# Expert biases split during w_o, slot lists read in one transfer per expert, six weight loads at the expert start, last tiles' routing in another order

## The chip, the cores and the metric

One core of a Trainium2 chip runs the whole layer. The metric is the device time of one execution in microseconds. The kernel before takes 2818.05 us, the median of three runs (2815.62 to 2819.49).

## The reference

Input x is (1, 1024, 1024): 1024 tokens of width 1024. After a mixer of two attention branches (a neighbourhood attention and a grouped-query attention), whose outputs are merged and multiplied by w_o, a mixture of experts follows. Cut to what the change touches:

```
x  = x + gt1 * rmsnorm(merge_branches(...) @ ..., g_post_mix)      # ends with the product by w_o
h2 = rmsnorm(x, g_pre_ffn) * (1 + sc2) + sh2
logits = h2 @ w_router + b_router                # 32 experts
top_logits, top_e = top_k(logits, 4)             # 4 experts for each token
top_w = softmax(top_logits)
for each expert e, for its tokens:               # 4096 assignments in all
    gu  = h2[tok] @ w_gu[e] + b_gu[e]            # 1024 x 2048
    act = (clip(gu_lin, -7, 7) + 1) * (min(gu_glu, 7) * sigmoid(1.702 * min(gu_glu, 7)))
    f[tok] += top_w * (act @ w_dn[e] + b_dn[e])  # 1024 x 1024
x  = x + gt2 * rmsnorm(f, g_post_ffn)
```

Everything is float32.

## The kernel before

A float32 product is made of three matmuls of a shorter type: each operand is split into hi and lo, and hi·hi, hi·lo and lo·hi are summed. ScalarE makes the hi of a weight piece (a copy, L1494), VectorE the lo (a subtraction, L1503).

The program runs through projections, attention, the product by w_o with the routing, the experts, and a final norm. A scheduler does not reorder it: each engine executes its instructions in the order in which the code issues them, and SP (SyncE) issues the DMAs of its queue in that order too. An instruction that waits holds back all that stands behind it on its engine.

**w_o and routing** (about 1000 to 1170 us). Eight tiles j of 128 tokens, each in two column chunks of 512 (ch = 0, 1). TensorE's product goes to a PSUM buffer z, and `evac` takes its sum of squares on ScalarE (L1203, Square) and multiplies it by a row on VectorE (L1205). An object `Post` carries a tile on in steps, which the loop interleaves with later tiles by a written list: s0 and s1 (norm, residual, the x2 store), s2 (second norm, the h2 store L1020), p0 (eight transposes of h2 and two copies to h2T, L1030), p1 (router product, L1036 and L1041, top four, softmax maximum), p2 (slot numbers), p3 (exponential L1277, weights, and four indirect DMAs from GpSimd, L1284, which write token and weight to their slots in DRAM, `slots_d`). For j from 4 to 6, tile j's list runs p1 of tile j−2, and p2 and p3 of j−3, behind its chunk 0, and s0 of j, p0 of j−1, then s1 and s2 of j behind its chunk 1. Behind tile 7's chunk 1 the rest has a list of its own.

**Experts** (about 1170 us to the end). 32 positions p. Even positions are wide experts (mode T, 304 slots at first, then fewer), odd ones narrow (64 or 128 slots). `slots(p)` reads which tokens an expert has from `slots_d`, by SP, one DMA for each 128 slots into buffers named slot, of which there are 12 (L1521), and for mode T a bias column (L1525). `gather(p)` fetches the token rows by an indirect DMA on GpSimd (L1534), `xtr(p)` transposes them (L1589). Steps U (gate and up, four for a position) and D (down, two) each take four weight pieces of 512 KB. A piece is loaded by SP (L1482) into one of 6 raw buffers, and split into 8 hi and 7 lo buffers. Between two wide experts steps alternate: U(p+1,0), U(p,2), U(p+1,1), U(p,3), U(p+1,2), D(p,0), U(p+1,3), D(p,1), D(p+1,0), U(p+2,0), D(p+1,1), U(p+2,1). The product of a T step is taken out of PSUM by ScalarE (gx, L1729) and VectorE (L1735). The output rows y are written back by indirect DMAs that take the token numbers from the slot buffer (f_d<-y, L1829).

`prepare(p)` calls `slots(p+2)`, `xtr(p)` and later `gather(p+1)`; it runs behind U(p−2,3) for even p and behind D(p−2,0) for odd p.

The biases of all experts (b_all, 32 rows of 3072) are needed from the first narrow step on, as hi in 32 partitions and lo in the next 32. At the expert start three DMAs on ScalarE's queue (L1852) read 1024 columns each, twice, into 64 partitions; ScalarE copies them to bhl (L1860) and VectorE subtracts (L1861).

Of the kernel before, what the change touches and what calls it, by code (L numbers as in the profile page):

```python
# [970 lines left out]
class Post:  # L971
# [22 lines left out]
    def s1(self):  # L994
        b, y = self.b, self.y
        nc, wk, V = b.nc, b.wk4, b.nc.vector
        r = self.r
        V.reciprocal(r[:, 1:2], r[:, 0:1])
        sq = b.w4.tile([P, D], F32, name="sq4", bufs=1)
# [38 lines left out]
    def p1b(self):  # L1038
        b, ps = self.b, self.lps
        for k in range(4, 8):  # L1040
            b.nc.tensor.matmul(ps[:, :32], self.hT[:, k, :], b.wr[:, k, :], start=False, stop=k == 7)  # L1041
        self.p2, self.p3 = b.route(self.t, ps)
# [6 lines left out]
class Tail(Build):  # L1049
# [65 lines left out]
    def phase4(self):  # L1115
# [56 lines left out]
        self.ctx3.close()  # L1172
        ws = ExitStack()
        wo["p"] = self.pool(ws, "wo")
        w4 = self.w4 = self.pool(es, "w4", 2, **R)
# [22 lines left out]
        def evac(ps, j, ch):  # L1198
# [3 lines left out]
            sq = w4.tile([P, D], F32, name="sq4", bufs=1)  # L1202
# [20 lines left out]
        for j in range(2, 8):  # L1223
            for ch in range(2):
                ps = self.tp4()
                for q in range(4):
                    gemm(ps, j, q, hl[8 + 2 * q + ch])
                evac(ps, j, ch)
                if ch == 0:
                    order = early.get(j, ((j - 2, "p1"), (j - 3, "p2"), (j - 3, "p3")))  # L1230
                elif j < 7:
                    order = ((j, "s0"),) + early.get(j + .5, ((j - 1, "p0"),)) + ((j, "s1"), (j, "s2"))
                else:
                    order = ((7, "s0"), (6, "p0"), (7, "s1"), (5, "p2"), (7, "s2"), (5, "p3"), (6, "p1"), (7, "p0"),
                             (7, "p1a"), (6, "p2"), (7, "p1b"), (6, "p3"), (7, "p2"), (7, "p3"))
# [9 lines left out]
    def route(self, t, ps):  # L1245
# [29 lines left out]
        def p3():  # L1275
            e4 = wk.tile([P, 4], F32, name="e4")
            nc.scalar.activation(e4, m8[:, 0:4], AF.Exp, bias=sm[:, 0:1], scale=1.0, accum_out=sm[:, 1:2])  # L1277
            data = wk.tile([P, 4, 2], F32, name="data")
# [10 lines left out]
        return p2, p3  # L1289
# [141 lines left out]
class Moe2(Tail):  # L1431
    def moe(self):
# [6 lines left out]
        es = self.early = ExitStack()  # L1439
        bhl = self.pool(es, "bia").tile([P, 3072], F32R, name="bhl")  # L1440
# [73 lines left out]
        def slots(p):  # L1514
            if p >= NE:
                return
            e = ereg("sync", p)
            SL[p] = []
            for a, n in tiles(p):
                sl = xgp.tile([P, 2], I32, name="slot", bufs=12)  # L1520
                nc.sync.dma_start(sl[:n], self.slots_d[ds(e * STRIDE + a, n), :])  # L1521
                SL[p].append(sl)
            if mode[p] == "T":
                b = xgp.tile([P, 24], F32, name="bcol", bufs=3)
                nc.sync.dma_start(b, A["b_col"][ds(e, 1)].rearrange("a p c -> p (a c)"))  # L1525
# [306 lines left out]
        def prepare(p):  # L1832
# [3 lines left out]
            slots(p + 2)  # L1836
            xtr(p)
# [7 lines left out]

        raw_b = []

        def load_biases():
            src = A["b_all"]
            for i in range(3):  # L1850
                r = wk.tile([P, D], F32, name="y5", bufs=3)
                nc.scalar.dma_start(r[:64], bass.AP(tensor=src.tensor, offset=src.offset + i * 1024,  # L1852
                                                    ap=[[0, 2], [3072, 32], [1, 1024]]))
                raw_b.append(r)

        def split_biases():
            G.memset(f(bhl[64:P]), 0.0)
            for i, r in enumerate(raw_b):
                cs = slice(i * 1024, i * 1024 + 1024)
                ACT.activation(bhl[0:64, cs], r[:64], AF.Copy)  # L1860
                V.tensor_tensor(out=bhl[32:64, cs], in0=r[32:64], in1=f(bhl[32:64, cs]), op=ALU.subtract)  # L1861
# [208 lines left out]
```

## Time and profile before

| | |
|---|---|
| median of three runs | 2818.05 us |
| the profiled execution | 2821.09 us |
| its span in the trace | 2819.5 us |
| mean granted TensorE clock | 0.977 of 2.4 GHz |
| TensorE busy | 2669.4 us (95%) |
| VectorE busy | 1958.6 us (69%) |
| ScalarE busy | 1591.3 us (56%) |
| GpSimd busy | 567.0 us (20%) |

TensorE's share of 95% is a mean. The page's second part cuts the span into 40 slices of 70 us and gives the busy tenths of each: only in the first slices, in slice 17 (about 1130 to 1200 us, between w_o and the experts) and in the last does TensorE fall under nine tenths, and in slice 17 its granted clock falls too.

```profile
PE   6899999999999999489999999999999999999993
PEclk9999999999999999699999999999999999999996
DMA  6224551502232343467787888888889889998896
```

### The profile page before, as it was taken

The numbers are of one execution on the slowest core, as the hardware profiler recorded it, in microseconds if no ns is written. First come the engines' busy times: TensorE is split into PE (matmuls) and PEld (weight loads), VectorE is DVE, ScalarE is ACT, GpSimd is POOL, SyncE is SP. The second block draws the span as 40 slices with busy tenths as digits, with TensorE's granted clock in tenths as the row PEclk, the third lists the DMA queues.
The fourth block names the chain that finished last, engine by engine and source line by source line (L and its number), as shares of the span: only waits on it lengthen the run. The fifth ranks groups of instructions, "written<-read, shape, count | busy, mean of one in ns | idle before, by whom it ended". The sixth has DMA issues, their size and how long they took to land. (4 is left out here: it accounts for less than half of the span.)

```text
span 2819.5 us, 44191 instructions
## 1 busy us (share of the span) xinstructions
PE 2669.4 (95%) x15564; PEld 2231.0 (79%) x15564; DVE 1958.6 (69%) x3148; ACT 1591.3 (56%) x2485; POOL 567.0 (20%) x495
## 2 busy tenths in 40 slices
PE   6899999999999999489999999999999999999993
PEld 3788887555677778488988899999999898998892
DVE  3722322777777546477877888888888888888895
ACT  3421212555577324356676666677677777777773
POOL 2310001666544222301011011011001100111001
PEclk9999999999999999699999999999999999999996
DMA  6224551502232343467787888888889889998896
GB/s 236 73 95 177 187 197 45 161 23 42 49 72 50 113 157 128 123 210 230 266 280 247 273 291 268 279 291 292 268 295 304 290 285 306 313 312 298 298 313 224
DMA packets 195618, 589.36 MB, mean 209 GB/s; under 512 B 48049, under 2 KB 54785, under 8 KB 195313
## 3 DMA queue, kind: packets, MB, share of 16 engines
q1 hardware_dynamic: 172443, 519.85, 54.4%
q0 software_dynamic: 19808, 65.27, 8.3%
q8 instruction: 123, 2.02, 0.3%
q10 hardware_dynamic: 3142, 1.40, 0.2%
q14 instruction: 102, 0.84, 0.1%
HBM read 528.74 MB, written 59.00 MB: 208 GB/s over the span
## 5 line engine op out<-in xcount | busy, mean ns | idle before, releaser
L1503 DVE TENSOR_TENSOR lo<-raw,hi 128x1024 fp32r<-128x1024 f32 x768 | 919.2, 1219 | 170.5 <-ACT hi L1494 74.8
L1494 ACT ACTIVATE hi<-raw 128x1024 fp32r<-128x1024 f32 x768 | 800.4, 1054 | 189.9 <-PE g L1657 82.9
L1657 PE MATMUL g<-xT,hi 128*128 128x320 f32 (+10 forms) x1792 | 518.2, 331 | 0.0
L1658 PE MATMUL g<-xT,lo 128*128 128x256 f32 x1792 | 483.6, 280 | 0.0
L1657 PEld LDWEIGHTS g<-xT,hi 128*128 128x128 f32 x1792 | 336.5, 188 | 10.8
L1658 PEld LDWEIGHTS g<-xT,lo 128*128 128x128 f32 x1792 | 338.4, 189 | 2.3
L1829 POOL DMA_INDIRECT f_d<-y,slot x34 | 59.9, 1762 | 1246.9 <-ACT y L1817 1105.4
L1657 PE MATMUL g<-aT,hi 128*128 128x288 f32 (+10 forms) x896 | 260.5, 333 | 0.0
L1658 PE MATMUL g<-aT,lo 128*128 128x256 f32 x896 | 241.9, 280 | 0.0
L1633 PE MATMUL g<-hi,xN 128*128 128x512 f32 x512 | 204.3, 399 | 0.0
L1634 PE MATMUL g<-lo,xN 128*128 128x512 f32 x512 | 202.4, 395 | 0.0
L174 DVE TENSOR_TENSOR wlo<-raw,whi 128x1024 fp32r<-128x1024 f32 x33 | 42.1, 1288 | 218.7 <-ACT whi L173 218.5
L1632 PE MATMUL g<-hi,xN 128*128 128x512 f32 x448 | 182.7, 408 | 0.0
L1657 PEld LDWEIGHTS g<-aT,hi 128*128 128x128 f32 x896 | 168.2, 188 | 5.2
L1658 PEld LDWEIGHTS g<-aT,lo 128*128 128x128 f32 x896 | 169.3, 189 | 0.6
L859 ACT ACTIVATE p<-S 128x512 f32<-128x512 f32 x160 | 94.2, 596 | 103.8 <-PE S L858 99.0
L613 DVE TENSOR_REDUCE mn<-S 128x1 f32<-128x512 f32 x180 | 100.8, 593 | 66.3 <-PE S L612 65.9
L400 PE MATMUL mm<-hTh,whi 128*128 128x512 f32 (+1 forms) x416 | 123.7, 385 | 1.7 <-ACT whi L173 1.7
L400 PE MATMUL mm<-hTh,wlo 128*128 128x512 f32 (+1 forms) x416 | 123.2, 383 | 0.0
L400 PE MATMUL mm<-hTl,whi 128*128 128x512 f32 (+1 forms) x416 | 123.0, 383 | 0.0
L1634 PEld LDWEIGHTS g<-lo,xN 128*128 128x128 f32 x512 | 96.4, 188 | 22.7
L1633 PEld LDWEIGHTS g<-hi,xN 128*128 128x128 f32 x512 | 96.4, 188 | 19.3
(413 smaller groups left out, 5804.0 us busy)
## 6 DMA issues: line engine op xcount, KB each, us to landing
raw<-in_w_gu_dram SPq DMA_DIRECT2D x509, 512.0 KB, 5.0
raw<-in_w_dn_dram SPq DMA_DIRECT2D x256, 512.0 KB, 4.5
raw<-in_w_mod_dram SPq DMA_DIRECT2D x40, 512.0 KB, 4.5
raw<-in_w_in_dram SPq DMA_DIRECT2D x34, 512.0 KB, 4.5
x<-in_x_dram SPq DMA_DIRECT2D x16, 512.0 KB, 5.4
sig_d<-stg POOLq DMA_DIRECT2D x16, 512.0 KB, 2.9
sig<-sig_d SPq DMA_DIRECT2D x8, 1024.0 KB, 4.9
kraw<-ka_d SPq DMA_DIRECT2D x16, 320.0 KB, 6.3
```

What stands on the lines that cost most here:

```text
L174: (G if i == 0 else V).tensor_tensor(out=lo, in0=r, in1=f(hi), op=ALU.subtract)
L400: T.matmul(ps[:, :n], w[:, ks], h[:, k, a:a + n], start=k == 0 and pi == 0, stop=k == KT - 1 and pi == 2)
L613: nc.vector.tensor_reduce(out=u.mn[:, i, j:j + 1], in_=ps[:, :n], op=ALU.min, axis=AX.X)
L859: nc.scalar.activation(u.p[t // 2][:, t % 2 * 512:t % 2 * 512 + 512], ps, AF.Exp, scale=-1.0)
L1494: ACT.activation(hi, raws[i], AF.Copy)
L1503: V.tensor_tensor(out=lo, in0=raws.pop(i), in1=f(his[pieces[i]]), op=ALU.subtract)
L1632: T.matmul(ps[:m], x[:, kk, P:P + m], hi[:, cs], start=False, stop=False)
L1633: T.matmul(ps[:m], x[:, kk, :m], hi[:, cs], start=False, stop=False)
L1634: T.matmul(ps[:m], x[:, kk, :m], lo[:, cs], start=False, stop=kk == 7)
L1657: T.matmul(ps[:, :2 * c], hi[:, cs], x[:, kk, :], start=first, stop=False)
L1658: T.matmul(ps[:, :256], lo[:, cs], x[:, kk, :256], start=False, stop=last)
L1829: G.indirect_dma_start(out=self.f_d, out_offset=bass.IndirectOffsetOnAxis(ap=SL[p][xi][:n, 0:1], axis=0), in_=Y[p][xi][:n], in_offset=None ...
```

## The change

- **Biases.** `biases(i)`, called behind the steps of tiles 3, 4 and 5, loads one third of b_all by SP, copies and subtracts; the bhl buffer is made before w_o. The DMA stands on SP behind the tile's h2 store, and on ScalarE the copy stands ahead of the next tile's Square. The scratch of the Squares (never read) moves to the ring "raw" of the earlier stage, from which the bias DMA's landing buffer is taken too.
- **Slot lists.** One DMA reads all slots of a position into one buffer of three columns, of which there are 5. The first two lists are read by GpSimd, behind the scatters; the bias columns have a function of their own on SP.
- **Expert start.** SP issues six weight loads at once; four rounds of hi, lo and a further load follow, then `prepare(0)`, then four hi and three lo.
- **Last tiles.** p3 is cut in two, the exponential (p3e) and the rest (p3d). Tile 5's exponential moves up behind tile 7's chunk 0; a dummy Exp behind s1 of tile 7 fixes where the activation table is loaded; p2 and the rest of p3 of tile 5 move ahead of s1 of tile 7, and p3 of tile 6 ahead of p1b of tile 7.

```
         sq = b.w4.tile([P, D], F32, name="sq4", bufs=1)      # before, in s1 and evac
+        sq = b.ring.tile([P, D], F32, name="raw")
...
+        def biases(i):
+            if i == 0:
+                G.memset(f(bhl[64:P]), 0.0)
+            src = A["b_all"]
+            r = self.ring.tile([P, D], F32, name="raw")
+            nc.sync.dma_start(r[:64], bass.AP(tensor=src.tensor, offset=src.offset + i * D,
+                                              ap=[[0, 2], [3072, 32], [1, D]]))
+            cs = slice(i * D, i * D + D)
+            ACT.activation(bhl[0:64, cs], r[:64], AF.Copy)
+            V.tensor_tensor(out=bhl[32:64, cs], in0=r[32:64], in1=f(bhl[32:64, cs]), op=ALU.subtract)
...
                 if ch == 0:
                     order = early.get(j, ((j - 2, "p1"), (j - 3, "p2"), (j - 3, "p3")))
+                    if j == 7:
+                        order += ((5, "p3e"),)
...
-                    order = ((7, "s0"), (6, "p0"), (7, "s1"), (5, "p2"), (7, "s2"), (5, "p3"), (6, "p1"), (7, "p0"),
-                             (7, "p1a"), (6, "p2"), (7, "p1b"), (6, "p3"), (7, "p2"), (7, "p3"))
+                    order = ((7, "s0"), (6, "p0"), (5, "p2"), (5, "p3d"), (7, "s1"), (7, "s2"), (6, "p1"), (7, "p0"),
+                             (7, "p1a"), (6, "p2"), (6, "p3"), (7, "p1b"), (7, "p2"), (7, "p3"))
                 for t, x in order:
                     getattr(tiles[t], x)()
+                    if (t, x) == (7, "s1"):
+                        ACT.activation(self.spacer2, self.eps[0:1], AF.Exp)
...
+                if ch == 1 and 3 <= j <= 5:
+                    biases(j - 3)
...
-        def slots(p):
+        def slots(p, eng="sync"):
...
-            for a, n in tiles(p):
-                sl = xgp.tile([P, 2], I32, name="slot", bufs=12)
-                nc.sync.dma_start(sl[:n], self.slots_d[ds(e * STRIDE + a, n), :])
+            e, nt = ereg(eng, p), len(tiles(p))
+            sl = xgp.tile([P, 3, 2], I32, name="slot", bufs=5)
+            getattr(nc, eng).dma_start(sl[:, :nt], self.slots_d[ds(e * STRIDE, nt * P), :].rearrange("(a p) c -> p a c", p=P))
+            SL[p] = [sl[:, i] for i in range(nt)]
...
-        load(2)
-        slots(0)
+        load(N_RAW)
+        slots(0, "gpsimd")
         gather(0)
-        load(3, "gpsimd")
-        split_hi(2)
-        split_lo(2)
-        load_biases()
-        slots(1)
+        slots(1, "gpsimd")
+        columns(0)
+        for _ in range(4):
+            split_hi()
+            split_lo()
+            load()
         prepare(0)
         while cold or chains:
             advance()
-        load(2)
-        split_hi(3)
+        split_hi(4)
         split_lo(3)
-        split_biases()
-        split_hi(3)
-        split_lo(2)
```

**ScalarE in w_o.** The first piece is ScalarE's order before, from tile 3's second norm (the Square of y, its square root) over the two Squares of tile 4's chunks to tile 3's h2T. "waits" names the engines or DMA lanes whose semaphore an instruction waits for.

```order
L1004 ACTIVATE sq4_9300,s24_9301<-y_9164 128x1024 [waits DVE_49,Activation_49]
L982 ACT_TABLE_LOAD
L982 ACTIVATE r4_9307<-s24_9301,eps_8243 128x1 [waits Activation_49]
L1203 ACTIVATE sq4_9341,ss_9338<-z_9312 128x512 [waits PE_49]
L1277 ACT_TABLE_LOAD
L1277 ACTIVATE e4_9376,sm_9261<-m8_9251,sm_9261 128x4
L1203 ACTIVATE sq4_9415,ss_9338<-z_9390 128x512 [waits PE_49,Activation_49]
L982 ACT_TABLE_LOAD
L982 ACTIVATE r4_9420<-s4_9418,eps_8243 128x1 [waits DVE_49]
L1030 ACTIVATE h2T_9422<-z_9423 128x512 [waits PE_49]
```

The same place after the change:

```order
L1004 ACTIVATE raw_9305,s24_9306<-y_9168 128x1024 [waits DVE_49]
L982 ACT_TABLE_LOAD
L982 ACTIVATE r4_9312<-s24_9306,eps_8243 128x1 [waits Activation_49]
L1191 ACTIVATE bhl_8848<-raw_9318 64x1024 [waits DMAHW0_49]
L1222 ACTIVATE raw_9351,ss_9348<-z_9322 128x512 [waits PE_49]
L1303 ACT_TABLE_LOAD
L1303 ACTIVATE e4_9269,sm_9266<-m8_9256,sm_9266 128x4
L1222 ACTIVATE raw_9425,ss_9348<-z_9400 128x512 [waits PE_49,Activation_49]
L982 ACT_TABLE_LOAD
L982 ACTIVATE r4_9430<-s4_9428,eps_8243 128x1 [waits DVE_49]
L1030 ACTIVATE h2T_9432<-z_9433 128x512 [waits PE_49]
```

The copy to bhl, which waits for a DMA lane, now stands between tile 3's square root and the Square of tile 4's first chunk; the square root of tile 4 and the h2T copies of tile 3 follow behind it.

**SP late in the pair of positions 4 and 5.** Before, SP's queue around the slot read for position 9 (slot) and the weight loads behind it:

```order
L1482 DMA raw5_13739<-in_w_dn_dram 128x1024 [waits DMAHW6_49,DVE_49]
L1482 ISA
L1482 DMA raw5_13752<-in_w_gu_dram 128x1024 [waits DMAHW7_49,DVE_49,Activation_49]
L1460 TENSOR_LOAD erow_10005
L1460 ISA x2
L1521 ISA
L1521 DMA slot_13763<-slots_d_103 128x2 [waits DMASW5_49,DMASW2_49]
L1482 ISA
L1482 DMA raw5_13798<-in_w_gu_dram 128x1024 [waits DMAHW0_49,DVE_49]
L1482 ISA
L1482 DMA raw5_13827<-in_w_gu_dram 128x1024 [waits DMAHW1_49,DVE_49]
```

And after the change:

```order
L1509 DMA raw5_13737<-in_w_gu_dram 128x1024 [waits DMAHW1_49,DVE_49,Activation_49]
L1509 ISA
L1509 DMA raw5_13750<-in_w_gu_dram 128x1024 [waits DMAHW2_49,DVE_49]
L1487 TENSOR_LOAD erow_10023
L1487 ISA x2
L1546 ISA
L1546 DMA slot_13761<-slots_d_103 128x2 [waits DMASW3_49,DMASW4_49,DMASW0_49,Activation_49]
L1509 ISA
L1509 DMA raw5_13796<-in_w_gu_dram 128x1024 [waits DMAHW3_49,DVE_49]
L1509 ISA
L1509 DMA raw5_13825<-in_w_gu_dram 128x1024 [waits DMAHW4_49,DVE_49]
```

One more weight load stands ahead of the read than before. The read's waits (DMASW lanes, GpSimd's DMAs) are before those of scatters of older positions; after the change they are the lanes of the scatters of position 4, whose slot buffer it takes, and of ScalarE.

**ScalarE behind it.** Before, the split of the first weight piece loaded behind that read (raw5_13798) and the gx evacuation of step U(6,0):

```order
L1494 ACTIVATE hi5_13748<-raw5_13739 128x1024 [waits DMAHW4_49,DVE_49]
L1573 ACTIVATE xN_13765<-t5_13788 128x4x128 [waits PE_49]
L1494 ACTIVATE hi5_13794<-raw5_13752 128x1024 [waits DMAHW5_49,DVE_49]
L1573 ACTIVATE xN_13765<-t5_13817 128x4x128 [waits PE_49]
L1494 ACTIVATE hi5_13823<-raw5_13798 128x1024 [waits DMAHW7_49,DVE_49]
L1494 ACTIVATE hi5_13850<-raw5_13827 128x1024 [waits DVE_49,DMAHW0_49,PE_49,Activation_49]
L1729 ACTIVATE gx_13864<-g5_13770,bcol_12184 128x224 [waits PE_49]
L1729 ACTIVATE gx_13864<-g5_13770,bcol_12184 128x224
L1729 ACTIVATE gx_13875<-g5_13771,bcol_12184 128x224 [waits PE_49]
```

And after the change, where that piece is raw5_13796:

```order
L1601 ACTIVATE xN_13763<-t5_13786 128x4x128 [waits PE_49]
L1521 ACTIVATE hi5_13792<-raw5_13737 128x1024 [waits DMAHW7_49,DVE_49]
L1601 ACTIVATE xN_13763<-t5_13815 128x4x128 [waits PE_49]
L1521 ACTIVATE hi5_13821<-raw5_13750 128x1024 [waits DMAHW0_49,DVE_49]
L1521 ACTIVATE hi5_13848<-raw5_13796 128x1024 [waits DVE_49,DMAHW2_49,PE_49,Activation_49]
L1757 ACTIVATE gx_13862<-g5_13768,bcol_12184 128x224 [waits PE_49]
L1757 ACTIVATE gx_13862<-g5_13768,bcol_12184 128x224
L1757 ACTIVATE gx_13873<-g5_13769,bcol_12184 128x224 [waits PE_49]
L1757 ACTIVATE gx_13873<-g5_13769,bcol_12184 128x224
```

The split of the first piece behind the read, which waits for its DMA, now stands directly ahead of the gx evacuation; before, one other split stood between.

## Rows read from the trace of the kernel before

**Rows 1.** Windows: us, busy of each engine (instructions), TensorE's clock, DMA share, GB/s.
```profile
1094.00:1102.10 8.10, 8.10 (x42) 6.81 (x42) 4.14 (x19) 2.86 (x6) 4.60 (x9) 1.00 0.40 130
1208.00:1216.00 8.00, 4.58 (x34) 4.34 (x32) 2.83 (x3) 3.45 (x4) 0.00 (x0) 1.00 0.22 84
2500.00:2589.00 89.00, 89.00 (x585) 80.59 (x584) 78.49 (x108) 67.64 (x101) 8.82 (x8) 1.00 0.90 309
```
**Rows 2.** Timeline, TensorE: start us, us, engine, line, operation, out<-in, count, idle before.
```profile
1142.13 0.40 PE L1194 MATMUL z<-wo15h,zl 128*128 128x512 f32 x1
...
1195.90 0.62 PE L1660 MATMUL g<-xT,hi 128*128 128x304 f32 x1
...
1236.59 0.40 PE L1624 MATMUL g<-bhl,oneh 128*128 128x512 f32 x1
```
**Rows 3.** Timeline of one w_o tile, SP, ScalarE and TensorE.
```profile
1094.20 0.32 SPq L1020 DMA_DIRECT2D h_d<-h  x1
...
1100.14 0.60 ACT L1203 ACTIVATE sq<-z 128x512 f32<-128x512 f32 x1 [5.21 <-PE z L1194]
...
1102.34 1.06 ACT L1030 ACTIVATE h2T<-z 128x512 f32<-128x512 f32 x2
...
1106.29 0.97 PE L1036 MATMUL z<-wr,h2T 128*128 128x32 f32 x8
...
1114.30 0.60 ACT L1203 ACTIVATE sq<-z 128x512 f32<-128x512 f32 x1 [5.42 <-PE z L1194]
```
**Rows 4.** Timeline, ScalarE, the third bias copy.
```profile
1212.55 1.06 ACT L1860 ACTIVATE bhl<-y 64x1024 fp32r<-64x1024 f32 x1 [5.79 <-DMA y<-in_b_all_dram]
```
**Rows 5.** DMA, 1176 to 1178 us, ScalarE's queue: packets, MB, share of sixteen engines.
```profile
q10 hardware_dynamic: 18, 0.07, 13.0%
```
**Rows 6.** DMA issues, whole span: count, KB each, median us to landing.
```profile
raw<-in_w_gu_dram SPq DMA_DIRECT2D x509, 512.0 KB, 5.0
...
raw<-qb_d SPq DMA_DIRECT2D x16, 256.0 KB, 3.5
```
**Rows 7.** Timeline, hand-over from routing to the first expert.
```profile
1159.18 0.98 POOL L1284 DMA_INDIRECT slots_d<-data,sl  x1 [3.92 <-DVE sm L1280]
...
1168.08 0.97 POOL L1284 DMA_INDIRECT slots_d<-data,sl  x1 [0.22 <-issue]
...
1172.60 1.61 SPq L1521 DMA_DIRECT2D slot<-slots_d  x3
...
1175.45 1.00 POOL L1534 DMA_INDIRECT xg<-h_d,slot  x1 [6.40 <-DMA slot<-slots_d]
...
1182.27 0.88 POOL L1534 DMA_INDIRECT xg<-h_d,slot  x1 [0.67 <-issue]
...
1191.96 0.63 PE L1589 MATMUL t<-ident,xg 48*128 48x48 f32 x4 [0.59 <-DMA xg<-h_d,slot]
```
**Rows 8.** Timeline, ends of positions 2 and 26.
```profile
1445.12 0.39 PE L1657 MATMUL g<-xT,hi 128*128 128x512 f32 x1
...
1445.79 1.73 POOL L1829 DMA_INDIRECT f_d<-y,slot  x1 [6.65 <-ACT hi L1494]
...
2587.72 0.33 SPq L1521 DMA_DIRECT2D slot<-slots_d  x1
...
2596.60 1.33 POOL L1829 DMA_INDIRECT f_d<-y,slot  x1 [7.71 <-DVE lo L1503]
...
2598.59 0.65 ACT L1729 ACTIVATE gx<-g,bcol 128x144 f32<-128x144 f32 x2
...
2605.22 0.30 PE L1657 MATMUL g<-xT,hi 128*128 128x288 f32 x1
```
**Rows 9.** DMA issues at those two scatters: count, us to landing.
```profile
f_d<-y,slot POOLq DMA_INDIRECT x1, 5.0
...
f_d<-y,slot POOLq DMA_INDIRECT x1, 6.9
```
**Rows 10.** The scatters' line (L1829) over the span.
```profile
DMA to landing us min/median/max: 3.1/8.8/11.3
```

More of the change, by code (lines that the diff above doesn't have):

```diff
@@ L998, in s1 @@
         V.reciprocal(r[:, 1:2], r[:, 0:1])
-        sq = b.w4.tile([P, D], F32, name="sq4", bufs=1)
+        sq = b.ring.tile([P, D], F32, name="raw")
         s2 = wk.tile([P, 2], F32, name="s24", bufs=4)
@@ L1041, in p1b, with p3 @@
             b.nc.tensor.matmul(ps[:, :32], self.hT[:, k, :], b.wr[:, k, :], start=False, stop=k == 7)
-        self.p2, self.p3 = b.route(self.t, ps)
+        self.p2, self.p3e, self.p3d = b.route(self.t, ps)
+    def p3(self):
+        self.p3e()
+        self.p3d()
     def p1(self):
@@ L1172, in phase4 @@
         self.ctx3.close()
+        self.early = ExitStack()
+        bhl = self.bhl = self.pool(self.early, "bia").tile([P, 3072], F32R, name="bhl")
         ws = ExitStack()
         wo["p"] = self.pool(ws, "wo")
+        def biases(i):
[8 more added lines that the diff above has]
+            V.tensor_tensor(out=bhl[32:64, cs], in0=r[32:64], in1=f(bhl[32:64, cs]), op=ALU.subtract)
         w4 = self.w4 = self.pool(es, "w4", 2, **R)
@@ L1201, in evac @@
             y, ss = tiles[j].y, tiles[j].ss
-            sq = w4.tile([P, D], F32, name="sq4", bufs=1)
+            sq = self.ring.tile([P, D], F32, name="raw")
             ACT.activation(sq[:, :512], ps, AF.Square, accum_out=ss[:, ch:ch + 1])
@@ L1273, in p2, with p3e, p3d @@
             V.tensor_tensor(out=self.cum, in0=self.cum, in1=mk[:, None, :].to_broadcast([P, 2, 32]), op=ALU.add)
-        def p3():
-            e4 = wk.tile([P, 4], F32, name="e4")
+        e4 = wk.tile([P, 4], F32, name="e4")
+        def p3e():
             nc.scalar.activation(e4, m8[:, 0:4], AF.Exp, bias=sm[:, 0:1], scale=1.0, accum_out=sm[:, 1:2])
+        def p3d():
             data = wk.tile([P, 4, 2], F32, name="data")
@@ L1288, in p3 @@
                     self.tc.declare_no_dep(self.scat[-1].ins, o.ins, reason="slots of other assignments")
-        return p2, p3
+        return p2, p3e, p3d
     def counts(self, wk):
@@ L1438, in moe @@
         N_HI, N_LO, N_RAW = 8, 7, 6
-        es = self.early = ExitStack()
-        bhl = self.pool(es, "bia").tile([P, 3072], F32R, name="bhl")
+        es, bhl = self.early, self.bhl
         rawp = self.pool(es, "raw5", N_RAW)
@@ L1512, in tiles, with columns @@
             return [(a, min(P, c - a)) for a in range(0, c, P)]
-        def slots(p):
+        def slots(p, eng="sync"):
             if p >= NE:
                 return
-            e = ereg("sync", p)
-            SL[p] = []
-            for a, n in tiles(p):
-                sl = xgp.tile([P, 2], I32, name="slot", bufs=12)
-                nc.sync.dma_start(sl[:n], self.slots_d[ds(e * STRIDE + a, n), :])
-                SL[p].append(sl)
-            if mode[p] == "T":
+            e, nt = ereg(eng, p), len(tiles(p))
+            sl = xgp.tile([P, 3, 2], I32, name="slot", bufs=5)
+            getattr(nc, eng).dma_start(sl[:, :nt], self.slots_d[ds(e * STRIDE, nt * P), :].rearrange("(a p) c -> p a c", p=P))
+            SL[p] = [sl[:, i] for i in range(nt)]
+        def columns(p):
+            if p < NE and mode[p] == "T":
                 b = xgp.tile([P, 24], F32, name="bcol", bufs=3)
-                nc.sync.dma_start(b, A["b_col"][ds(e, 1)].rearrange("a p c -> p (a c)"))
+                nc.sync.dma_start(b, A["b_col"][ds(ereg("sync", p), 1)].rearrange("a p c -> p (a c)"))
                 BC[p] = b
@@ L1836, in prepare @@
             slots(p + 2)
+            columns(p + 2)
             xtr(p)
@@ L1843, in prepare @@
             cold.append(then())
[L1846 to L1861, printed above, removed]
-        load(2)
-        slots(0)
-        gather(0)
-        load(3, "gpsimd")
-        split_hi(2)
-        split_lo(2)
-        load_biases()
-        slots(1)
+        load(N_RAW)
+        slots(0, "gpsimd")
+        gather(0)
+        slots(1, "gpsimd")
[4 more added lines that the diff above has]
+            load()
         prepare(0)
```

## The prediction

> **What bounds the kernel now.** I read the windows first, then TensorE's timeline over the joint between two stages, then the chain through one w_o tile, one hand-over and one pair of experts, and last the DMA issues. In the w_o stage TensorE is busy 8.10 of 8.10 us while VectorE is busy 4.14, and late in the expert stage it is busy 89.00 of 89.00 us with the DMA engines at 0.90 [rows 1]. So in both stages TensorE sets the time, and whatever makes it wait is paid whole. Between them it idles: w_o's last matmul is at 1142.13, the first expert product at 1195.90 [rows 2]. That joint is a chain of latencies (scatter of slots, slot read, gather, transpose), and there the change can win. The first two expert steps are slow too: 40.7 us (1195.90 to 1236.59, [rows 2]) for 192 matmuls; at the pace of the second window, 34 in 4.58 us busy or 0.135 each [rows 1], they need 25.9.
>
> **A. The expert start.** Before, six raw buffers fill in two lots, and three of the loads stand on GpSimd's queue behind the gathers; now all six go out on SP as soon as the buffers exist, and four are split ahead of the first transposes. The bias copy, which before still waited for its transfer at 1212.55 [rows 4] with the splits of weights queued behind it on ScalarE, is gone from here. Of the 14.8 us lost in the first two steps I keep 3 for TensorE's slower clock after idling and for the first loads, and take 11.8 as gained.
> The rest is the slot path. Tile 6's scatters began at 1159.18, 3.92 us after the queue fell empty, and eight in a row ended at 1169.05 (1168.08 + 0.97). With tile 6's routing put ahead of tile 7's half I estimate that the run starts 2.7 us sooner (most of the 3.92) and ends at 1166.3. From the scatters' end the slot read took 3.6 to issue (1172.60) and 2.9 more to the first gather (1175.45): now about 1172.8. The third gather was issued 6.8 after the first, since each waited for its own slot list; with one list the three follow each other at about 1 us, so the third goes at 1174.8 and, with the same 9.7 to landing (1182.27 to 1191.96), lands at 1184.5 [rows 7]. Ten weight loads, 5.2 MB, now run beside it, for which I take 1.5 back: 1186, so 6 us sooner. Sum of A: −18, from −12 (the gathers starve beside the loads) to −23 (they do not, and the clock costs nothing).
>
> **B. The biases in w_o.** Per transfer: one DMA, one ScalarE copy of 1.06 [rows 4], one VectorE subtract, about 1.2. The work itself lies beside TensorE. The wait does not: ScalarE runs in program order, and the copy stands directly ahead of the Square that evacuates the next product, with a wait on the transfer. The transfer is issued behind the h2 store at 1094.20 [rows 3], so at about 1094.55. When does it land? The trace shows the same access on ScalarE's queue: 18 packets in 2 us at 13.0% of sixteen engines, that is 9 per us on 2.1 engines [rows 5]. 256 KB in 4 KB packets are 64, so 7.1 us, and I add 2.6 for start and completion, near the 2.85 from a slot read's issue to the gather that waits for it [rows 7]: 9.7. The bounds are 3.5, which a 64-partition load of the same size took [rows 6], and 14, if the 0.40 that other traffic takes of the DMA engines in w_o [rows 1] comes off its rate.
> The Trainium skill, "DMA: Bandwidth & Descriptors", section "Why a DMA increments its semaphore by 16 and not by 1", says that a DMA uses as many engines, up to 16, as divide the slowest dimension of both sides; the source's is 2 here, and the trace's 2.1 engines agree. The same page's "Anatomy of one DMA" fits 2.0 us plus bytes over 436 GB/s, an estimate of 2.6 us for 256 KB, and by it B would be nothing; the 9 packets per us speak against it.
> What is late: from landing, the copy 1.06, the subtract 1.2, VectorE's row of evacuation and routing (4.4: the 4.14 of the first window [rows 1] and small gaps), the square root 0.3 and the two h2T copies 1.06 [rows 3] make 8.1, with hand-overs 8.3. TensorE's router product read h2T at 1106.29 [rows 3]; now h2T is ready at 1094.55 + 9.7 + 8.3 = 1112.55: a stall of 6.3, or landing time minus 3.4. For the next two tiles the chain closes on itself. From the h2T copies' start (1102.34) to the next bias transfer are 6.4 (1094.55 plus the period 14.16 between 1100.14 and 1114.30, [rows 3]). A round is 9.7 + 8.3 − 1.06 + 6.4 = 23.3 against 14.16: 9.1 more, twice. Sum of B: 6.3 + 18.2 = 24.5, taken as +25; with landing in 3.5 it is 0 to 6 (the rounds 3 longer each), with 14 it is +37.
>
> **C. Slot lists in five buffers.** Before there were twelve buffers of 128 rows; now five, each for a whole expert. The read for position p+5 takes over the buffer of p, and p's scatters read their row numbers there until they have landed. For even p this read is issued just after p's last output step. SP issues in order, so it stands still until the last scatter of p has landed, and the weight loads stand behind it. In SP's order the wait changes from old scatters to the newest ones, and in ScalarE's order the split of the next load stands directly ahead of the gx evacuation. There are 14 such reads (positions 5, 7, ... 31).
> The price at p = 26: SP reached the read at 2587.72; the last scatter began at 2596.60 and landed 6.9 later, 2603.5 [rows 8, 9]. From there the next load needs 0.6 to issue, 5.0 to land [rows 6], its ScalarE split 1.06, and then, ScalarE being in order, the gx evacuation 0.65 [rows 8] that frees the product's PSUM buffer, with some 0.5 of VectorE: 7.8. TensorE wanted that buffer at 2605.22 [rows 8]; 2603.5 + 7.8 = 2611.3, so 6 late. Done so for all 14: 2.9 for the first, 13.6 for the second (1445.79 + 5.0 + 7.8 against 1445.12, [rows 8, 9]), 5.3 on average for twelve, together 80. But while SP stands still no weights fly, and scatters land faster: the fastest took 3.1 against a median of 8.8 [rows 10]. I take 3.8 off the landing and 0.5 off the first load's: 0 for the first, 9 for the second, 1 for each of the twelve. Sum of C: +20, from 5 (only the second pair shows) to 80.
>
> The tail's remaining swaps (an exponential earlier, one activation-table load more) lie in A's chain and are in its 2.7. Scratch for the squares moved to another ring: nothing, since it is written and never read, unless ScalarE waits for a raw weight in it (under 1).
>
> **Sum.** −18 + 25 + 20 = +27 on the profiled execution's 2821.09 (span 2819.5): 2848. That execution lies 3.0 above the median of the three runs, 2818.05; so **2845**.
>
> **Rivals.**
> 1. Only the gain shows: the bias transfer lands within 3.5 us (for it: the 64-partition load; against: the row of 9 packets per us), and scatters land so fast without weights that SP loses nothing (for it: 3.1; against: the second scatter of a tile still starts some 9 us after SP arrives). 2818 − 18 = 2800. Faster.
> 2. The scatters land no faster, so C costs its 80: for it, packets of loads already queued still run; 2818 − 18 + 25 + 80 = 2905. This is the slow end.
> 3. C is hidden, six raw buffers carrying TensorE across: 2818 − 18 + 25 = 2825. Against it: TensorE waits not for the load but for the evacuation behind its split.
> 4. B is hidden, C as forecast: 2818 − 18 + 20 = 2820, no change that a measurement of this kernel can tell (within 0.2%, 5.6 us).
>
> **Chances.** Forecast 0.60, rival 1 0.15, rival 2 0.10, rival 3 0.08, rival 4 0.07. Slower by over 0.2% takes the forecast, rival 2 and some of 3, less a little for a forecast whose terms come out low together: 0.73. Within 0.2%: 0.09. Faster: rival 1 and a little of the rest, 0.18. The forecast's own range, from the bounds taken moderately, is 2822 to 2890; half of rival 1 goes in at the lower end, rival 2 stays out: 2800 to 2890.
>
> **What would show it.** A: first expert product near 1215 (1195.90 − 6 + 25), and steps U(0,0) and U(0,1) in about 29 us. B: three gaps of TensorE in w_o ahead of the router product of tiles 3, 4, 5, of 6 to 9 us, and ScalarE idle ahead of the bias copy released by the bias DMA; landing near 9.7. C: SP's wait of 5 to 10 us at every second slot read released by a scatter, a dip in weight traffic, and TensorE gaps at the second step of even positions, large at position 4. I am wrong if these gaps are absent, above all if the bias lands within 4 us, or if scatters landing early let SP go on before TensorE needs the buffer.

## The result, and the profile after

The changed kernel takes 2958.08 us (median of 6 runs, 2948.71 to 2962.04) against 2818.89 us for the kernel before on the same chip: ratio 1.0489, 95% interval 1.0471 to 1.0506. The forecast was slower, 2845 us, with a range to 2890: the direction was right, the size was not. The profiled execution spans 2956.1 us against 2819.5, so 136.6 us are to be found.

The page of the kernel after, second part, in slices of 74 us:

```profile
PE   6999999999999997699899999999999899999993
PEclk8999999999999997799999999999999999999996
```

TensorE's tenths hide it: the slices of the expert stage read 9 and 8 where they were 9. The windows of one long stretch tell more. Columns as in [rows 1]; first the kernel after, then the kernel with six slot buffers (below), whose TensorE, VectorE and ScalarE are busy there as long as before to within 0.4%. Behind the bounds stand the length, the busy time of TensorE, of its weight loads, of VectorE, ScalarE and GpSimd, then TensorE's granted clock, the DMA share and GB/s:

```profile
1500.00:2700.00 1200.00, 1124.95 (x6668) 1021.13 (x6667) 929.73 (x1233) 784.60 (x1149) 107.57 (x77) 0.97 0.82 265
```
```profile
1500.00:2700.00 1200.00, 1193.90 (x7315) 1084.19 (x7314) 1014.23 (x1344) 864.83 (x1259) 122.05 (x87) 1.00 0.88 290
```

TensorE lies idle for 75 of 1200 us instead of 6, the DMA engines carry 265 instead of 290 GB/s, and the granted clock is 0.97 instead of 1.00.

**w_o.** The kernel after, timeline of SP, ScalarE and TensorE around the first bias, to be held against [rows 3], and TensorE's two later waits and its last product of w_o (before at 1142.13, [rows 2]):

```profile
1095.18 0.65 SPq L1188 DMA_DIRECT2D raw<-in_b_all_dram  x1
...
1105.38 1.06 ACT L1191 ACTIVATE bhl<-raw 64x1024 fp32r<-64x1024 f32 x1 [12.17 <-DMA raw<-in_b_all_dram]
...
1112.81 1.92 PE L1036 MATMUL z<-wr,h2T 128*128 128x32 f32 x8 [5.75 <-ACT h2T L1030]
...
1134.75 1.51 PE L1036 MATMUL z<-wr,h2T 128*128 128x32 f32 x8 [3.41 <-ACT h2T L1030]
...
1156.56 1.92 PE L1036 MATMUL z<-wr,h2T 128*128 128x32 f32 x8 [4.18 <-ACT h2T L1030]
...
1168.61 0.40 PE L1213 MATMUL z<-wo15h,zl 128*128 128x512 f32 x1
```

Windows of the same trace, while ScalarE stands at the bias copy and behind each of the three waits:

```profile
1100.50:1105.30 4.80, 4.80 (x27) 4.07 (x26) 0.00 (x0) 0.00 (x0) 0.00 (x0) 1.00 0.13 51
...
1112.80:1116.00 3.20, 3.19 (x15) 3.19 (x16) 2.85 (x4) 1.89 (x4) 2.92 (x4) 0.50 0.45 160
1134.70:1138.00 3.30, 3.25 (x18) 3.25 (x18) 2.94 (x4) 1.93 (x4) 2.93 (x4) 0.58 0.43 162
1156.50:1160.00 3.50, 3.44 (x17) 3.45 (x17) 3.15 (x4) 2.87 (x8) 2.98 (x5) 0.50 0.40 150
```

ScalarE stands 12.17 us at the bias copy, which starts 10.2 after the transfer's issue; late in that time the DMA engines are at 0.13 of sixteen, or 2.1 engines. TensorE waits three times, 13.3 us in all, and the eight router matmuls behind each wait take 1.5 to 1.9 us instead of 0.97: the granted clock there is 0.50 to 0.58, all or most of the time the lower of its two levels (1.2 of 2.4 GHz). w_o ends 26.5 us later; 25.9 of them come between its first product and its last (112.9 us instead of 87.0).

**The hand-over.** The kernel after, GpSimd (last scatter, first slot list, first and third gather) and TensorE's first expert product, against [rows 7] and [rows 2]:

```profile
1192.44 0.97 POOL L1312 DMA_INDIRECT slots_d<-data,sl  x1 [0.22 <-issue]
...
1198.78 0.82 POOL L1546 DMA_DIRECT2D slot<-slots_d  x1 [5.38 <-ACT hi L1521]
...
1204.77 1.00 POOL L1562 DMA_INDIRECT xg<-h_d,slot  x1 [5.17 <-DMA slot<-slots_d]
...
1207.34 0.88 POOL L1562 DMA_INDIRECT xg<-h_d,slot  x1 [0.30 <-issue]
```
```profile
1217.86 0.62 PE L1688 MATMUL g<-xT,hi 128*128 128x304 f32 x1
...
1247.12 0.40 PE L1652 MATMUL g<-bhl,oneh 128*128 128x512 f32 x1
```

The gathers follow each other at 1.3 us instead of spreading over 6.8, but the first begins 12.3 after the last scatter's start, not 7.4. From w_o's last product to the first expert product are 49.3 us (53.8 before), and the first two steps take 29.3 (40.7 before). The three gathers land after 4.4 to 6.1 us, where before they took 9.1 to 9.6.

**A pair of experts.** The kernel after at the end of position 20, GpSimd, SP, ScalarE and TensorE, to be held against [rows 8], and the landing of that scatter, after and before:

```profile
2424.49 1.36 POOL L1857 DMA_INDIRECT f_d<-y,slot  x1 [8.20 <-DVE lo L1530]
...
2428.16 0.34 SPq L1546 DMA_DIRECT2D slot<-slots_d  x1
2428.76 3.43 SPq L1509 DMA_DIRECT2D raw<-in_w_gu_dram  x5
...
2434.03 1.06 ACT L1521 ACTIVATE hi<-raw 128x1024 fp32r<-128x1024 f32 x1 [9.38 <-DMA raw<-in_w_gu_dram]
2435.00 1.23 ACT L1757 ACTIVATE gx<-g,bcol 128x160 f32<-128x160 f32 x4
...
2436.24 0.63 PE L1685 MATMUL g<-xT,hi 128*128 128x320 f32 x1 [3.20 <-DVE gx L1763]
```
```profile
f_d<-y,slot POOLq DMA_INDIRECT x1, 3.5
```
```profile
f_d<-y,slot POOLq DMA_INDIRECT x1, 5.5
```

The scatter lands at 2428.0, the slot read goes at 2428.16, and the load behind it reaches ScalarE at 2434.03; the gx evacuation stands behind that split, and TensorE waits 3.20. That is the mechanism of the forecast's part C. What the forecast missed is in the next windows of the same trace: while SP stands, while TensorE waits, in the second step of the position, and in its third:

```profile
2422.00:2428.00 6.00, 6.00 (x45) 5.88 (x45) 3.05 (x3) 1.65 (x3) 3.04 (x4) 1.00 0.17 23
...
2434.00:2440.00 6.00, 3.76 (x19) 3.76 (x19) 4.21 (x7) 5.39 (x9) 0.00 (x0) 0.72 0.90 354
...
2436.24:2446.30 10.06, 10.06 (x65) 10.02 (x66) 9.99 (x13) 8.03 (x10) 3.19 (x2) 0.86 0.89 285
...
2452.00:2465.30 13.30, 9.83 (x67) 9.60 (x66) 11.89 (x18) 8.69 (x12) 0.00 (x0) 0.91 1.02 411
```
```profile
2461.76 0.44 PE L1723 MATMUL t<-ident,gx 128*128 128x128 f32 x2 [3.47 <-DVE gx L1717]
```

For 6 us the DMA engines move 23 GB/s. In the second step TensorE is busy throughout at a granted clock of 0.86; that alone is the 1.4 us by which the step is longer than with six buffers. Some 25 us after the dip the DMA engines are at 1.02 and 411 GB/s (a share counts the whole time of the packets that began in the window, so it can pass 1), VectorE is busy 11.89 of 13.30, and TensorE idles again, for 3.47, at an evacuation on VectorE. Against the trace with six buffers, step by step, the loss is some 56 us up to the start of the second step of an even position, 26 in that step, and 47 in the third step of the position; the forecast had only the first of the three.

### The profile page after: what moved, and what is told of

It is laid out like the page before. It is cut to its first block, busy times and chain, and to the rows that moved or that the text cites. A ratio compares the mean times of both kernels' runs of the same rounds, so it can differ in the third digit from the quotient of the medians.

```text
span 2956.1 us, 44137 instructions
## 1 busy us (share of the span) xinstructions
PE 2716.0 (92%) x15564; PEld 2272.8 (77%) x15564; DVE 1954.8 (66%) x3148; ACT 1584.8 (54%) x2486; POOL 572.7 (19%) x494
## 5 line engine op out<-in xcount | busy, mean ns | idle before, releaser
L1685 PE MATMUL g<-xT,hi 128*128 128x320 f32 (+10 forms) x1792 | 545.6, 344 | 54.4 <-DVE gx L1763 54.4
L1686 PE MATMUL g<-xT,lo 128*128 128x256 f32 x1792 | 499.6, 289 | 0.0
L1685 PEld LDWEIGHTS g<-xT,hi 128*128 128x128 f32 x1792 | 354.2, 198 | 71.0 <-DVE gx L1763 60.0
L1686 PEld LDWEIGHTS g<-xT,lo 128*128 128x128 f32 x1792 | 354.4, 198 | 1.9
L1763 DVE TENSOR_TENSOR gx<-g,gx 128x368 f32<-128x368 f32 (+10 forms) x112 | 59.9, 534 | 158.4 <-ACT gx L1757 157.7
```

What stands on the lines that cost most here:

```text
L1685: T.matmul(ps[:, :2 * c], hi[:, cs], x[:, kk, :], start=first, stop=False)
L1686: T.matmul(ps[:, :256], lo[:, cs], x[:, kk, :256], start=False, stop=last)
L1763: V.tensor_tensor(out=x, in0=ps[:, :, :c], in1=x, op=ALU.add)
```

## The experiments

Times are medians, each with the kernel before on the same chip (2818.0 to 2819.6 us).

**One more slot buffer** (`slots6`).

```
-            sl = xgp.tile([P, 3, 2], I32, name="slot", bufs=5)
+            sl = xgp.tile([P, 3, 2], I32, name="slot", bufs=6)
```

> The kernel after, with 6 instead of 5 slot buffers, nothing else. Theory (SP's wait for the scatters that still read the buffer makes the whole loss of the expert stage, by late evacuation, the slower clock behind it and a debt of weight loads): the second steps of even positions no longer stall, the 124 us lost behind the first two steps vanish, and the time is 2819 + 10.6 = 2830 us (2822 to 2838). Rival 1 (the transfer of a whole list in 8-byte rows is itself what holds up the weight loads): nothing or little changes, 2940 to 2960. Rival 2 (half of it is the new load order at the start, which leaves the weights later all along): 2870 to 2910.

2831.19 us (1.0047, 1.0034 to 1.0060). One buffer of 24 bytes in a partition is worth 127 us, and both rivals fall. SP's waits from 1480 to 2700 us, the kernel after and then this one (engine, line, waited for: us in total, times, longest; a read that waits for two scatters counts twice, so the 19 are eleven reads, of 13.0 us each):

```profile
SPq L1509 <- DVE lo L1530: 564.4, 350, 7.5
SPq L1546 <- DMA f_d<-y,slot: 142.7, 19, 14.5
```
```profile
SPq L1509 <- DVE lo L1530: 655.6, 419, 4.7
SPq L1509 <- DVE aN L1604: 74.9, 52, 2.6
```

The wait for the scatters is gone from SP's list; with six buffers an odd position takes over the buffer of an odd one, whose scatter is long past.

**The wait on another queue** (`slots5_gpsimd`): five buffers, GpSimd reads the lists.

```
-        def slots(p, eng="sync"):
+        def slots(p, eng="gpsimd"):
```

> The kernel after with 5 buffers, but every slot list read by GpSimd instead of SP: the wait for the newest scatters stays, on another queue, with no weight loads behind it. Theory (the weight loads behind the wait are what costs): near the run with 6 buffers, 2830 us, up to 2850 if the gathers that now stand behind the wait on GpSimd come late. Rival (a list that arrives late costs by itself, through its gather and the next expert's start): over 2900.

2823.78 us (1.0019, 1.0009 to 1.0029). The wait is still there, as GpSimd's list in the same stretch shows, and costs nothing:

```profile
POOL slot L1546 <- DMA f_d<-y5n,slot: 103.4, 11, 10.9
...
POOL slot L1546 <- DMA f_d<-y,slot: 44.9, 9, 6.2
```

The list is even read later: about 2 us ahead of the second step's first product, where the kernel after reads it about 8 ahead. So not the wait, nor a late list, but the weight loads queued behind it are what costs. That this run is 7 us below the one with six buffers on SP was not followed up.

**Only the slot lists** (`before_slots5`): the kernel before with the one transfer and five buffers, on SP.

```
-            for a, n in tiles(p):
-                sl = xgp.tile([P, 2], I32, name="slot", bufs=12)
-                nc.sync.dma_start(sl[:n], self.slots_d[ds(e * STRIDE + a, n), :])
...
+            sl = xgp.tile([P, 3, 2], I32, name="slot", bufs=5)
+            nc.sync.dma_start(sl[:, :nt], self.slots_d[...])
...
```

> The kernel before with only the slot lists changed: one transfer for a position into one of 5 buffers, all on SP, the start of the experts and w_o as before. Theory: it loses in the expert stage what the kernel after lost there, 2819 + 124 = 2943 us (2920 to 2955). Rival 2 (half of it is the new load order at the start): 2860 to 2900.

2936.32 us (1.0421, 1.0401 to 1.0442): +118, nearly the whole loss, with nothing of the rest.

**Biases by two transfers** (`slots6_bias16`), with six buffers.

```
-            nc.sync.dma_start(r[:64], bass.AP(..., ap=[[0, 2], [3072, 32], [1, D]]))
+            for h in range(2):
+                nc.sync.dma_start(r[h * 32:h * 32 + 32], bass.AP(..., ap=[[3072, 32], [1, D]]))
```

> The kernel after with 6 slot buffers, and each bias transfer in w_o made as two of 32 partitions each (slowest dimension 32 instead of 2). Theory (the bias transfer lands late because it runs on two engines, and ScalarE's copy waits for it): it lands in 3 to 4 us, TensorE's three gaps in w_o go from 26 us in all to 0 to 6, and the time is 2830 - 23 = 2807 us (2800 to 2815). Rival (the wait is for the x load or the h2 store beside it on the same engines, not for the two engines): the bias still lands after 8 us or more and the time stays at 2825 to 2835.

2810.08 us (0.9972, 0.9962 to 0.9982), 21 less. Timeline of SP and ScalarE:

```profile
1092.85 1.20 SPq L1189 DMA_DIRECT2D raw<-in_b_all_dram  x2
...
1097.63 1.06 ACT L1192 ACTIVATE bhl<-raw 64x1024 fp32r<-64x1024 f32 x1 [6.73 <-DMA raw<-in_b_all_dram]
```

The same bytes land in 4.8 us instead of 10.2, later than the 3 to 4 expected here and still over the 3.4 that the forecast gave as the point from which a stall begins; w_o takes 93.1 us from its first product to its last, 6.2 more than before instead of 25.9.

**Split behind the evacuation** (`evac5`, `evac6`): with five and with six buffers.

```
-                if q < 3:
+                if q < (2 if late else 3):          # late: step 0 of even positions from 2 on
                     slot()
...
+            if late:
+                slot()
             slot()
```

> The kernel after (5 slot buffers, SP waits as there), but in the first step of the even positions from 2 on, the split of the next weight piece is issued behind the step's gx evacuation instead of ahead of it. Theory (TensorE waits at the second step because ScalarE, in order, stands at a split whose weights are late, and the evacuation stands behind it): the gaps at the start of the second step (56 us in all) and the slow clock behind them (some 24) go; what the late weights do one step later (some 40) stays: 2958 - 80 = 2878 us (2850 to 2910). Rival (TensorE waits for the weights themselves): no change, 2940 to 2965.

> The same exchange of split and evacuation with 6 slot buffers, as the control: without a wait on SP the exchange does little, 2831 us (2825 to 2840) by both theories.

2930.12 us and 2841.86 us. The price of five buffers falls from 127 to 88: 39 where I expected 80 (the time itself fell by 28). The gap at the second step went as expected, but about half of it came back one step later: against its control the third step loses 76 us instead of 47. In evac5, from the end of SP's wait to that later gap (2412 to 2430, then 2430 to 2446), and the gap itself on TensorE:

```profile
2412.00:2420.00 8.00, 8.00 (x48) 7.17 (x47) 3.46 (x6) 2.96 (x4) 0.00 (x0) 1.00 0.96 357
2420.00:2430.00 10.00, 10.00 (x62) 9.10 (x61) 8.89 (x10) 8.26 (x13) 3.89 (x2) 1.00 0.97 324
2430.00:2446.00 16.00, 11.27 (x70) 10.91 (x69) 14.40 (x22) 10.44 (x16) 0.00 (x0) 0.82 1.03 386
```
```profile
2441.85 0.69 PE L1723 MATMUL t<-ident,gx 128*128 128x128 f32 x2 [4.73 <-DVE gx L1717]
```

The DMA engines run without a pause for 34 us and TensorE still comes to a stop, at VectorE's work (14.40 of 16.00 us busy), which stands in order behind the late splits. The theory of the evacuation alone is too small. The exchange itself costs 11 us (the control), which I had not expected.

**Half the weight traffic** (`half5`, `half6`): a piece loads 512 of its 1024 columns, and the splits read these twice.

```
-                getattr(nc, eng).dma_start(r, src[ds(e, 1), j * 4 + q]...)
+                getattr(nc, eng).dma_start(r[:, :512], src[ds(e, 1), j * 4 + q, :, 0:512]...)
...
-                ACT.activation(hi, raws[i], AF.Copy)
+                ACT.activation(hi..., raws[i][:, None, :512].to_broadcast([P, 2, 512]), AF.Copy)
...
```

VectorE's subtraction reads the half twice in the same way. Half of the weights are left out, so the result is not the reference's, here and in the other runs with half loads.

> The kernel after with 5 slot buffers, but each expert weight piece loads only its first half (256 KB), which ScalarE and VectorE use twice: the same instructions on every engine, half the weight traffic, and a result that isn't the reference's. SP still waits for the scatters. Theory (the loss is a debt of weight loads, which the DMA engines, 0.90 busy, can't make up at once): with them half idle the debt is paid before TensorE needs it, and against the run with 6 buffers and half loads this loses little, 0 to 30 us. Rival (the loss is the wait itself, one landing of a weight load and ScalarE's split ahead of the evacuation): it still loses some 60 us or more.

> The same half loads with 6 slot buffers, as the control for the run before: 2790 to 2831 us by both theories, since TensorE sets the time of the expert stage.

2883.30 us and 2827.73 us: five buffers cost 56, between what the two theories gave. Over half of the price hangs on the weight traffic, and a part doesn't. But half loads change more than the work to be made up. In the traces, over the twelve pairs from position 4 on, SP's slot read comes 1.9 us earlier against the moment at which TensorE wants the buffer, and the load behind it reaches its split 0.8 us sooner; the gap at the second step falls by 2.6, from 3.7 to 1.1, which is those two together. So the second step's gap fell because the one wait got shorter; only the third step, 28 us instead of 47, speaks for the debt of loads.

**Half the splits too** (`hsplit5`, `hsplit6`): raw, hi and lo buffers of 512 columns, each used by the matmuls for both halves.

```
-                his[pieces[i]] = hi = hip.tile([P, 1024], F32R, name="hi5")
+                his[pieces[i]] = hi = hip.tile([P, 512], F32R, name="hi5")
...
-                            cs = slice(k * 512 + (gi * 2 + i) * P, k * 512 + (gi * 2 + i) * P + P)
+                            cs = slice((gi * 2 + i) * P, (gi * 2 + i) * P + P)
```

> 5 slot buffers; weight pieces loaded and split only in their first half (512 columns), TensorE's matmuls using that half twice, so that the DMA traffic and the splits on ScalarE and VectorE are halved and TensorE's work stays (the result isn't the reference's). Theory (the 56 us left with half loads are a debt of splits, VectorE being 0.85 busy): against the same with 6 buffers it loses under 20 us. Rival (they are the evacuation behind a late split, whatever the load of the engines): 40 to 60 us.

> The same with 6 slot buffers, as control: 2800 to 2828 us, TensorE setting the time.

2822.24 us and 2811.96 us: 10 us are left of 127, although SP still waits for nearly as long. SP's waits in hsplit5, 1480 to 2700 us, and its window:

```profile
SPq L1546 <- DMA f_d<-y,slot: 124.7, 18, 13.4
```
```profile
1500.00:2700.00 1200.00, 1194.58 (x7355) 1090.00 (x7354) 710.38 (x1349) 616.19 (x1265) 103.52 (x87) 1.00 0.55 159
```

VectorE is busy there for 710 of 1200 us, and 1014 with full splits and six buffers. The loss in the third step is gone.

**Both** (`evac_half5`, `evac_half6`): half loads, split behind the evacuation.

> 5 slot buffers, half loads (the first half used twice, the splits in full), and the split issued behind the gx evacuation in the first step of even positions. Theory (debt of splits): of the 56 us little goes, 35 to 55 left against its control. Rival (the evacuation behind the late split): under 20 us left.

> The same with 6 slot buffers, as control: some 10 us above half loads with 6 buffers alone, as with full loads, 2838 us.

2855.89 us and 2828.58 us: 27 left. Neither forecast (35 to 55, under 20) holds; the evacuation's order is worth 28 here and 39 with full loads. The control missed too: it was expected 10 us above half loads alone and lies 1 above, so the 11 us of the exchange are gone with half the weight traffic.

What five buffers cost, each against its own control with six:

| | split ahead of the evacuation | behind it |
|---|---|---|
| full loads and splits | 126.9 us | 88.3 us |
| half loads | 55.6 us | 27.3 us |
| half loads, half splits | 10.3 us | not run |

Where it is lost, from the step times of each trace against its control's (us, over all positions; the rest is 2 to 5 us the other way):

| | up to the start of the second step | in the second step | in the third step |
|---|---|---|---|
| full loads and splits | 56 | 26 | 47 |
| half loads | 22 | 6 | 28 |
| half loads, half splits | 13 | 4 | 0 |
| full loads, split behind | −1 | 16 | 76 |
| half loads, split behind | −1 | 10 | 26 |

**Only the biases** (`before_bias16`): the kernel before, biases in w_o by two transfers, all else as it was.

> The kernel before with only the biases moved into w_o, each as two transfers of 32 partitions; slot lists, loads at the expert start and tile order as before. w_o grows by some 4 us. Theory A1 (the first two expert steps were slow because ScalarE's bias copies waited for their transfers with the weight splits behind them): their 40.8 us fall to about 30, 2818 + 4 - 11 = 2811 us. Theory A2 (they were slow because three loads stood on GpSimd behind the gathers and only five were issued early): 38 us or more, 2820 us.

2807.92 us (0.9971, 0.9958 to 0.9985). TensorE, to be held against [rows 2], and GpSimd's last scatter and its gathers, against [rows 7]:

```profile
1145.88 0.40 PE L1210 MATMUL z<-wo15h,zl 128*128 128x512 f32 x1
...
1192.02 0.62 PE L1677 MATMUL g<-xT,hi 128*128 128x304 f32 x1
...
1221.70 0.40 PE L1641 MATMUL g<-bhl,oneh 128*128 128x512 f32 x1
```
```profile
1171.80 0.97 POOL L1302 DMA_INDIRECT slots_d<-data,sl  x1 [0.22 <-issue]
...
1178.63 1.00 POOL L1551 DMA_INDIRECT xg<-h_d,slot  x1 [5.86 <-DMA slot<-slots_d]
1179.94 0.97 POOL L1551 DMA_INDIRECT xg<-h_d,slot  x1 [0.30 <-issue]
1181.21 0.88 POOL L1551 DMA_INDIRECT xg<-h_d,slot  x1 [0.30 <-issue]
```

The first product comes 46.1 us after w_o's last (53.8 before), and the first two steps take 29.7 us (40.7 before). Theory A1 holds: the biases (their copies, or their transfers beside them; the run moves both) were what made the start slow, and new loads and new lists add next to nothing to it (29.3). The gathers go 1.3 us apart here too, with three separate lists as before, so it was not the one list that put them in a row.

**Copies one chunk later** (`bias_late`, and with the change's order of the last tiles `bias_late_tail`; `best` is the same copy in the kernel after with six buffers and lists read by GpSimd).

```
                 if ch == 1 and 3 <= j <= 5:
                     biases(j - 3)               # the two DMAs alone
+                if ch == 0:
+                    bsplit()                    # copy and subtract of the last transfer
```

> The kernel after with 6 slot buffers, all slot lists read by GpSimd, biases by two transfers of 32 partitions, and the bias copies put one chunk later on ScalarE, behind the next tile's first Square, where the transfer has landed. Theory: w_o keeps its pace of before (the 4 to 6 us that are left of the stalls go), and SP no longer issues slot reads (7 us as between the runs with 6 buffers on SP and 5 on GpSimd): 2810 - 5 - 5 = 2800 us (2795 to 2806). Rival (those 7 us were chance or the clock): 2805 us.

> The kernel before with only the biases moved into w_o, each as two transfers of 32 partitions, and with the copies one chunk later on ScalarE, where the transfer has landed. Theory: w_o takes no longer than before, so the 4 us that the run with the early copy lost there come back: 2808 - 4 = 2804 us (2800 to 2808), as fast as the version with every part of the change in it. Rival (new slot lists and new load order are worth something beside it): 2808 us, or slower than 2803.5 by 4 us or more.

> The same with the change's order of the last tiles. My forecast took 2.7 us for it: 2801 us. Rival (the slot list of tile 7, the last, sets the end of the scatters and comes no earlier): no change, 2804 us.

`best` 2803.52 us (0.9953, 0.9939 to 0.9968), `bias_late` 2802.71 (0.9941, 0.9925 to 0.9958), `bias_late_tail` 2800.06 (0.9929, 0.9913 to 0.9946), the fastest here. `best` lies between its theory (2800) and its rival (2805) and tells neither. In `best` the first gather starts 11.4 us after the last scatter's start, in `bias_late` 6.6, with w_o equally long in both: it is the new start that gives away what the early loads should bring. The first list is read 2.0 us later there and takes 2.8 us longer from its issue to the gather. Ten weight loads lie in the DMA queues beside it, but it is also read as one list and on GpSimd's queue; these were not separated. The 2.6 us of the tile order are near the forecast's 2.7 and near what runs scatter by, and the two intervals overlap; in the traces the last scatter starts 23.8 us after w_o's last product instead of 25.9.

## Why the prediction was wrong

- **A, the expert start, −18.** Right in sum: −4.5 in the hand-over and −11.4 in the first two steps. The 11.8 for the steps was close, and the cause I named beside the loads, the biases, carries nearly all of it (11.0 in `before_bias16`). In the hand-over I took 6, and that it came near is partly luck: the first list came 5 us later, for which I had taken 1.5, and the gathers, for which I had kept 9.7 to landing, landed after 4.4 to 6.1. The gathers in a row were there, but not because of the one list: with the biases gone from the start, three lists gave the same (`before_bias16`).
- **B, the biases in w_o, +25.** Right: +25.9 within w_o. Landing 10.2 for 9.7. The 2.6 that I set aside comes from a section of the Trainium skill on DMAs that GpSimd issues ("DMA: Bandwidth & Descriptors", "Anatomy of one DMA"), while SP issued this one; it did not come about. The sum is partly luck: the first stall is 6.0 for 6.3, but a round takes 21.9 us for 23.3, and 4.5 come behind the third wait, where I had nothing. Only 13.3 of the 25.9 are waits; the rest goes with the slower clock (0.80, 0.83 and 0.62 on average from each wait to the next or to w_o's end), which the sum does not have. That the two engines are the reason is shown by the 0.13 of sixteen above and by `slots6_bias16`. The Trainium skill, "DMA: Bandwidth & Descriptors", "Why a DMA increments its semaphore by 16 and not by 1", has it so (a DMA uses the largest number of engines up to 16 that divides the slowest dimension of both sides, here 2), and the 4.8 us with dimension 32 agree.
- **C, the slot buffers, +20.** Here it failed: 127 measured. Mechanism, place and count (14 reads) were right; the step that failed is "I take 3.8 off the landing and 0.5 off the first load's: 0 for the first, 9 for the second, 1 for each of the twelve", and with it that the sum ended at the second step's gap.
  The 3.8 was too much. It is what the scatter of position 26 (6.9, [rows 9]) lies above the fastest of all (3.1, [rows 10]), taken off all fourteen, and it came true at position 26 alone. The last scatters of the even positions landed 0.1 to 3.8 us sooner than before, 1.6 on average over the eleven whose landing both traces have, and the first load after them was no faster (4.8 to 6.3, for 5.0). With 1.6 for each of the 14, the bound of 80 becomes 58, an estimate from the same rows; the gaps measured at the second steps are 54, and the loss there is 56.
  The rest of the 127 the sum had at nothing, without a reason: 26 us in the second step, nearly all of it the slower clock behind the gap, and 47 in the third step. In my own first paragraph the DMA engines were at 0.90 and VectorE at 78.49 of 89.00 us [rows 1]: a chain with a tenth to spare can't make good a stop of 11 to 19 us before the next step needs it. I counted the loads that did not fly as help for the scatters and never as work still to be done. For the third step the runs show it: its 47 fall to 28 with half the weight traffic and to 0 with half the splits too, and rise to 76 when the evacuation no longer takes its part of the delay. How the 28 divide between the amount of VectorE's work and its order behind the late splits stays open.
- **Rival 2** (80) had the wait at its full length and the same gap: even at full length it was one wait, and its 2905 is 53 us short. **Rival 3** argued from the raw buffers, and they did not carry TensorE across. **Rivals 1 and 4** fall with the landing of 10.2 us and with the three waits in w_o.
- The range's upper end (2890) lay below even the bound of 80, which was left to rival 2; and the 80 priced the second step's gap alone, so it was no bound.

## What to carry to other kernels

Before a ring of buffers is cut, look at who reads a buffer last and at what stands behind the instruction that reuses it: a wait on a queue with nothing urgent behind it was free here, on the queue of the weight loads it cost 127 us. Price a stop of a feeding queue twice: by the one wait that follows, and as work to be made up, by the spare share of every engine on the chain. And look at the outermost dimension of a transfer: 256 KB with an outermost 2 took 10.2 us here, and 4.8 as two transfers with an outermost 32.

## What the runs showed that I had not expected

- An indirect scatter of token rows lands sooner when no weights fly, but not by much: the last scatter of position 20 in 3.5 us instead of 5.5, and 1.6 sooner on average over eleven positions. The median of 8.8 [rows 10] belongs mostly to the first scatter of a position, which still took 8.0 to 9.3 in the kernel after.
- After a stop the DMA engines were busy without a pause, at 1.02 of their share and 411 GB/s, and at 1.03 and 386 GB/s for 16 us in `evac5`. With six buffers the stage uses 0.88 and 290 GB/s on average, so little of their time was left to make up a stop with.
- Behind waits of 3 to 6 us TensorE's granted clock was lower for a time (0.50 to 0.58 for 3 us in w_o, 0.86 over a whole expert step in which TensorE was busy throughout), which made most of the waits in the expert stage dearer by one to three microseconds.
